# A Hymba encoder block on one core: part of the softmax shift moved from VectorE to accumulating DMAs, and loads moved from the GpSimd queue to the sync queue

## The chip, the cores and the metric

The kernel runs on one core of a Trainium2 chip. The metric is device time in microseconds (us) from launch to end; the median over runs counts. The span of a profiled execution is a little shorter than its time, since it runs from the first instruction to the last.

## The reference

One encoder layer over 2048 tokens and 16 meta tokens, all in float32, width 1024:

```python
h = concat([meta, x])                                   # 2064 x 1024
proj = rms_norm(h, g_mix) @ w_in                        # q (4 heads), k, v (2 heads of 128), u (512)
attn = softmax(rope(norm(q)) @ rope(norm(k)).T / sqrt(128)) @ v     # 2 query heads share a K/V head
four = real(fft2(u)) per 128-wide group, @ w_fourier
h = h + concat([rms_norm(attn), rms_norm(four)]) @ w_out
h = h + square(relu(rms_norm(h) @ w_up)) @ w_down       # 1024 -> 4096 -> 1024
out = rms_norm(h, g_final)[16:]
```

## The kernel before, in words

The work comes in stages: norm and input projections (until about 310 us of the profile), Fourier transform, output projection of the Fourier half (`out_f`), output projection of the attention half (`out_a`), and the MLP in two passes over 1024 tokens each (from about 1020 us), with seven products in place of eight blocks (forms "1" to "7", in `ORDER = "1265734"`). Most products are three float32r matmuls of high and low parts (`mm3`, lines 80 to 82).

Attention runs beside Fourier, `out_f` and `out_a`. It has 16 units: a unit is 256 query positions of two query heads that share one K/V head, so 512 columns. Its 2048 keys are 16 tiles of 128, held transposed (keys in the partitions): eight pairs, each one tile `S` of 128x1024, and a short tile for the meta tokens. For a unit:

- `scores`: three matmuls per key tile into a PSUM bank (two banks, tag "S"), a ScalarE copy into the half of `S` (L780), and once per pair a running maximum on VectorE (`M`, L783 and L786).
- `stats`: the maximum over keys by transposes (`pm_m`, `pd_m`), copied by ScalarE to `mb` (128x512, the same row in all partitions, L811).
- `softmax`: per pair a subtraction of `mb` on VectorE (L840), the exponential on ScalarE (L841), an addition into `acc` on VectorE (L845, L847) and four matmul passes with V into `o` (L849).
- `finish`: sums over keys, reciprocal, scaling, and a store to DRAM (`o_d`).

The scores of the next unit are computed while the softmax of the present one goes on. There are 11 buffers of `S`, eight of which one unit fills.

A scheduler of the framework sets the order on each engine's queue from the program's order and its own estimates; every queue then runs strictly in order. Five queues matter: PE (TensorE), DVE (VectorE), ACT (ScalarE), POOL (GpSimd: small tensor operations, and DMAs that it issues) and SP (sync: DMAs alone). Before, q, K (`kt`), V (`vn`, `vm`) of the units are loaded from DRAM by DMAs on POOL, since their tiles have another type (float32r) than the DRAM tensors. POOL also computes the reciprocal roots (`rs_f`, `rs_m`, `ers`) by which `out_f`, `out_a` and the final norm scale.

Between the two MLP passes, the second pass's seven operand forms of 2 MB each (`bf_tile`, from `f_d`) are loaded: six on SP, form 7 on POOL. Form 7's tile shares its memory (tag "e0") with rows of the first pass that are still being normed and stored at that time (`ers`, L1452; stores L1462 on POOL).

Of the kernel before, what the change touches and what calls it, by code (L numbers as in the profile page):

```python
# [13 lines left out]
AF = mybir.ActivationFunctionType  # L14
ALU = mybir.AluOpType
# [4 lines left out]
P = 128  # L20
# [11 lines left out]
NT = SEQ // P  # L32
# [3 lines left out]
MR = 96  # L36
# [13 lines left out]
P_BUFS = 5  # L50
S_BUFS = 11
A_BUFS = 5
ORDER = "1265734"
ISQ = 1.0 / math.sqrt(HD)


def f32v(ap):
    return ap.bitcast(F32)
# [26 lines left out]
def ins_of(x):  # L85
    return getattr(x, "ins", x)


def bc(ap, shape):
    return ap.broadcast_to(shape)  # L90
# [45 lines left out]
def encoder_block(ctx: ExitStack, tc: tile.TileContext, x, meta, w_in, w_f,  # L136
                  w_out, w_up, w_down, g_fin, g_cols, g_rows, c_id, c_rope, c_dft, c_even, c_odd, c_rem, out):
    nc = tc.nc
# [56 lines left out]
    q_d = [dram.tile([P, 2, NQ, 256], F32, name=f"q_d{b}") for b in range(8)]  # L195
    k_d = dram.tile([P, NKV, 2, SEQ + MR], F32, name="k_d")
    v_n = dram.tile([P, NKV, NT, P], F32, name="v_n")
    v_m = dram.tile([MR, NKV, P], F32, name="v_m")
    h_d = [dram.tile([P, D], F32, name=f"h_d{t}") for t in range(NT)]
    m_d = [dram.tile([P, KT, 512], F32, name=f"m_d{b}") for b in range(4)]  # L200
    f_d = {n: dram.tile([P, 2, 4, 512], F32, name=f"f_d{n}") for n in ORDER}

# [491 lines left out]
    def misc(name, shape=(P, 512)):  # L694
        return app.tile(list(shape), F32, name=name, tag="misc")


    KC = 4 * P
    KCP = 640

    def load_k(u, g, c):
        n = KC + (MR if c == 3 else 0)
        kt = ap.tile([P, 2, KCP if c == 3 else KC], R32, name=f"kt_{u}_{c}", tag=f"KT{c // 3}", bufs=1 if c == 3 else 3)
        nc.gpsimd.dma_start(kt[:, :, :n], k_d[:, g, :, c * KC:c * KC + n])
        return kt

    def load_v(u, g, c):
        if c == 4:
            vt = ap.tile([P, P], R32, name=f"vm_{u}", tag="VM", bufs=1)
            nc.gpsimd.dma_start(vt[:MR], v_m[:, g])  # L710
        else:
            vt = ap.tile([P, 4, P], F32, name=f"vn_{u}_{c}", tag="VT", bufs=4)
            nc.gpsimd.dma_start(vt, v_n[:, g, 4 * c:4 * c + 4])
        return vt

    o_d = [dram.tile([P, 2, NQ, 512], F32, name=f"o_d{b}") for b in range(4)]
# [12 lines left out]
    def attention():  # L729
# [5 lines left out]
        def load_q(u):  # L735
            b, g = units[u]
            q = ap.tile([P, 2, 2, 256], R32, name=f"q_{u}", tag="q", bufs=2)
            nc.gpsimd.dma_start(q, q_d[b][:, :, 2 * g:2 * g + 2])
            return q.rearrange("p l h n -> p l (h n)")

        def start(u, q=None):
            q = load_q(u) if q is None else q
            state[u] = dict(q=(q[:, 0], q[:, 1]), S=[], k=KV["k", u])
# [3 lines left out]
        def loads(kind, u, c):  # L747

            if u and units[u][1] == units[u - 1][1]:
                KV[kind, u] = KV[kind, u - 1]  # L750
            else:
                KV.setdefault((kind, u), []).append((load_v if kind == "v" else load_k)(u, units[u][1], c))
# [37 lines left out]
        def over_keys(x, name, op):  # L790

            ps = misc("pm_" + name, (P, 4, P))
            for a in range(4):
                nc.tensor.transpose(ps[:, a], x[:, a * P:(a + 1) * P], ident)
            r = ap2.tile([P, 4], F32, name="mx_" + name, tag="mx", bufs=2)
            nc.vector.tensor_reduce(r, ps, axis=AX.X, op=op)
            return r

        def rows_to_cols(vec, name):

            ps = misc("pd_" + name, (P, 4, P))
            for a in range(4):
                nc.tensor.transpose(ps[:, a], bc(vec[:, a:a + 1], [P, P]), ident)
            return ps.rearrange("p a e -> p (a e)")

        def stats(u):
            s = state[u]
            r = over_keys(s["M"], f"m{u}", ALU.max)
            yield
            mb = s["mb"] = ap2.tile([P, 512], F32, name=f"mb_{u}", tag="mb", bufs=2)  # L810
            nc.scalar.copy(mb, rows_to_cols(r, f"m{u}"))  # L811

        def softmax(u, i):

            s = state[u]
            nm = f"{u}_{i}"
            vt = KV["v", u]
            if i == NT:
                S = s["S"][-1][:MR]
                nc.vector.tensor_tensor(S, S, s["mb"][:MR], op=ALU.subtract)  # L820
                nc.scalar.activation(S, S, AF.Exp, scale=ISQ)
                hi = ap2.tile([P, 512], R32, name="ph_" + nm, tag="ph", bufs=1)
                acc = s["acc"]
                nc.scalar.copy(hi[:MR], S)
                nc.vector.tensor_tensor(hi[32:64], S[32:64], f32v(hi[32:64]), op=ALU.subtract)
                sm = s["sum"] = ap2.tile([P, 512], F32, name=f"sum_{u}", tag="pl", bufs=1)
                nc.vector.tensor_tensor(sm, acc[:, 0], acc[:, 1], op=ALU.add)
                nc.vector.tensor_tensor(sm[:META], sm[:META], S[:META], op=ALU.add)
                nc.tensor.matmul(s["O"], vt[4][:MR], hi[:MR], start=False, stop=True)
                return  # L830
            j = i // 2
            S = s["S"][j]
            if i == 0:
                s["acc"] = ap2.tile([P, 2, 512], F32, name=f"acc_{u}", tag="acc", bufs=1)
                s["O"] = app.tile([P, 512], F32, name=f"o_{u}", tag="O")
            acc = s["acc"]
            p = S
            if i % 2 == 0:
                mb = s["mb"].rearrange("p (o n) -> p o n", o=1).broadcast_to([P, 2, 512])
                nc.vector.tensor_tensor(S, S, mb, op=ALU.subtract)  # L840
                nc.scalar.activation(p, S, AF.Exp, scale=ISQ)  # L841
                return
            v = vt[j // 2]
            if j == 1:
                nc.vector.tensor_tensor(acc, s["S"][0], p, op=ALU.add)  # L845
            elif j > 0:
                nc.vector.tensor_tensor(acc, acc, p, op=ALU.add)  # L847
            for e in range(2):
                nc.tensor.matmul(s["O"], v[:, 2 * j % 4 + e], p[:, e], start=i + e == 1, stop=False)  # L849

        def finish(u):
# [25 lines left out]
            else:  # L877
                for h in range(2):
                    nc.vector.tensor_tensor(sqs[b], sqs[b], O[:, h * 256:(h + 1) * 256], op=ALU.add)

        q0 = load_q(0)
        for c in range(4):
            loads("k", 0, c)
# [7 lines left out]
        def more(upto):  # L891
            while ahead[0] < min(upto, total):
                w, i = divmod(ahead[0], K)
                if i == K // 2 and w < len(units) - 1:
                    start(w + 1)
                scores(w, i)
                loads_next("k", w, i)
                ahead[0] += 1
                if i == NT:
                    later.append(stats(w))  # L900
# [6 lines left out]
        for n in range(total):  # L907
            u, i = divmod(n, K)
            for g in list(later):
                if next(g, "end") == "end":  # L910
                    later.remove(g)
            softmax(u, i)
            loads_next("v", u, i)
            if i == NT:
                later.append(finish(u))
                next(later[-1])
            more(n + 1 + K + LEADT)
            yield
# [102 lines left out]
    def a_tile(name, dt=F32):  # L1021
        return mp.tile([P, 512], dt, name=name, tag="a", bufs=A_BUFS)

# [126 lines left out]
    BT = {}  # L1150

    def bf_tile(pool, name, **kw):
        t = BT[name] = pool.tile([P, 2, 4, 512], R32, name="bf" + name, **kw)
        BF[name] = [[t[:, e, k] for k in range(4)] for e in range(2)]
# [51 lines left out]
    def up_pass(p, sp, pc, UW, ready, first, hs, beside):  # L1206
# [8 lines left out]
        for g in range(8):  # L1215
            X, Y, p1, u2, p5, C = ({} for _ in range(6))

            def keep(name, q, t):
                nc.sync.dma_start(s_d[g // 2][:, ORDER.index(name), 2 * (g % 2) + q], t)

            for name in ORDER:
                hi, lo = ready.pop(0)
# [81 lines left out]
    def down_pass(p, sp, FIRST, hs):  # L1304
# [36 lines left out]
        def down_operands():  # L1341

            for g in range(4):
                raw, S, loads = {}, {}, []

                def stationary(name):
                    S[name] = []
                    for h in range(2):
                        r = dn.tile([P, 2, 512], F32, name=f"a{name}_{p}_{g}_{h}", tag="ar", bufs=a_bufs)
                        eng = nc.sync if g else nc.gpsimd  # L1350
                        loads[:] = [ins_of(eng.dma_start(r, s_d[g][:, ORDER.index(name), 2 * h:2 * h + 2]))]
                        S[name].append(r)
# [119 lines left out]
        for g in range(4):  # L1472
            X, Y = {}, {}
            last = g == 3
            for name in ORDER:
                (a0, b0), (a1, b1) = (lambda f: ((f[0], f[1]), (f[2], f[3])))(ready.pop(0))
# [134 lines left out]
    for name in "2165347":  # L1611
        if name == "7":
            bf_tile(ey, name, tag="e0")
        else:
            bf_tile(bfb, name)
    nc.gpsimd.dma_start(f32v(BT["7"]), f_d["7"])
    behind = nc.sync.dma_start(f32v(BT["1"]), f_d["1"])
    for name in "2U6534":
        with tc.issue_after(ins_of(behind)):
            if name == "U":  # L1620
                ready.append(next(UW))
            else:
                behind = nc.sync.dma_start(f32v(BT[name]), f_d[name])
# [109 lines left out]
```

## Time and profile before

| what | value |
|---|---|
| time, median of 3 runs | 2276.55 us (2273.15 to 2279.17) |
| profiled execution: time, span | 2273.03 us, 2271.2 us |
| busy: PE, DVE, ACT, POOL | 99%, 75%, 52%, 11% of the span |
| granted TensorE clock | 0.997 |
| DMA: queue q1 (issued by SP) | 307.98 MB, 40.1% of 16 engines |
| DMA: queue q0 (issued by POOL) | 57.37 MB, 8.0% of 16 engines |

Busy times come from one profiled execution. Matmuls are pipelined and their ends are modelled, so "PE busy" also holds a little waiting. A group's row reads: line, engine, operation, output<-inputs, shapes, count, busy us, mean ns of one, and the idle time of that engine just before it with what ended it.

### The profile page before, as it was taken

The numbers are of one execution on the slowest core, as the hardware profiler recorded it, in microseconds if no ns is written. First come the engines' busy times: TensorE is split into PE (matmuls) and PEld (weight loads), VectorE is DVE, ScalarE is ACT, GpSimd is POOL, SyncE is SP. The second block draws the span as 40 slices with busy tenths as digits, with TensorE's granted clock in tenths as the row PEclk, the third lists the DMA queues.
The fourth block names the chain that finished last, engine by engine and source line by source line (L and its number), as shares of the span: only waits on it lengthen the run. The fifth ranks groups of instructions, "written<-read, shape, count | busy, mean of one in ns | idle before, by whom it ended". The sixth has DMA issues, their size and how long they took to land.

```text
span 2271.2 us, 28115 instructions
## 1 busy us (share of the span) xinstructions
PE 2238.5 (99%) x10238; PEld 1772.9 (78%) x10238; DVE 1693.4 (75%) x2250; ACT 1178.0 (52%) x1997; POOL 245.6 (11%) x286
## 2 busy tenths in 40 slices
PE   9999999999999999999999999999989999999998
PEld 7888987766667666677888878888878888788887
DVE  6334589999999888888676769679655656696795
ACT  6443356665555566668555644334445555443343
POOL 2212120003223122010000020000100000200000
PEclk9999999999999999999999999999999999999999
DMA  6332252133343524367767575444674444864442
GB/s 204 88 107 78 76 156 81 51 94 113 102 154 117 193 87 136 126 255 241 254 223 247 210 268 194 159 129 148 234 304 166 154 152 154 307 200 158 127 138 84
DMA packets 191786, 367.40 MB, mean 162 GB/s; under 512 B 15760, under 2 KB 74768, under 8 KB 189984
## 3 DMA queue, kind: packets, MB, share of 16 engines
q1 hardware_dynamic: 170896, 307.98, 40.1%
q0 software_dynamic: 20608, 57.37, 8.0%
q8 instruction: 80, 1.31, 0.2%
q14 instruction: 58, 0.48, 0.1%
q10 hardware_dynamic: 144, 0.26, 0.0%
HBM read 236.28 MB, written 129.27 MB: 161 GB/s over the span
## 4 chain that ended last, share of the span: by engine, by line
PE 87%; DVE 6%; ACT 2%; issue 2%; POOL 1%; DMA 1%; SPq 0%; POOLq 0%; DVEq 0%; ACTq 0%
PE o L849 7%; PE ux L82 5%; PE ux L80 5%; PE ux L81 5%; PE dx L80 5%; PE dx L81 5%; PE dx L82 5%; PE uy L82 4%; PE uy L80 4%; PE uy L81 4%; PE dy L82 4%; PE dy L81 4%; PE dy L80 4%; PE s L80 2%; PE s L82 2%; PE s L81 2%
## 5 line engine op out<-in xcount | busy, mean ns | idle before, releaser
L70 ACT CAST ah<-a 128x1024 fp32r<-128x1024 f32 x108 | 112.9, 1049 | 261.3 <-PE dx L81 105.6
L849 PE MATMUL o<-S,vn 128*128 128x512 f32 x512 | 243.6, 596 | 3.7 <-ACT S L841 3.0
L80 PE MATMUL dx<-bh,ah 128*128 128x512 f32 x496 | 192.7, 388 | 1.3 <-DVE hs L1493 1.3
L780 ACT COPY S<-s 128x512 f32<-128x512 f32 x256 | 145.2, 585 | 92.4 <-PE s L82 72.8
L82 PE MATMUL dx<-bh,al 128*128 128x512 f32 x496 | 192.6, 388 | 0.0
L81 PE MATMUL dx<-bl,ah 128*128 128x512 f32 x496 | 192.5, 388 | 0.0
L80 PE MATMUL ux<-bf,wuh 128*128 128x512 f32 x448 | 175.5, 392 | 6.8 <-ACT wuh L70 6.8
L82 PE MATMUL ux<-bf,wul 128*128 128x512 f32 x448 | 175.0, 391 | 0.0
L81 PE MATMUL ux<-bf,wuh 128*128 128x512 f32 x448 | 175.0, 391 | 0.0
L840 DVE TENSOR_TENSOR S<-S,mb 128x1024 f32<-128x1024 f32 x128 | 155.4, 1229 | 11.9 <-ACT mb L811 11.8
L841 ACT ACTIVATE S<-S 128x1024 f32<-128x1024 f32 x128 | 135.1, 1063 | 43.0 <-DVE S L840 41.8
L80 PE MATMUL dy<-bh,ah 128*128 128x512 f32 (+1 forms) x388 | 151.2, 390 | 3.5 <-ACT ah L70 3.5
L82 PE MATMUL dy<-bh,al 128*128 128x512 f32 (+1 forms) x388 | 151.4, 390 | 1.6 <-DVE al L71 1.6
L71 DVE TENSOR_TENSOR al<-a,ah 128x1024 fp32r<-128x1024 f32 x108 | 131.3, 1220 | 27.1 <-ACT ah L70 26.8
L81 PE MATMUL dy<-bl,ah 128*128 128x512 f32 (+1 forms) x388 | 151.0, 389 | 0.0
L849 PEld LDWEIGHTS o<-S,vn 128*128 128x128 f32 x512 | 92.1, 189 | 74.6 <-issue 59.0
L80 PE MATMUL s<-q,kt 128*128 128x512 f32 (+1 forms) x272 | 145.2, 534 | 2.2 <-ACT S L780 1.9
L71 DVE TENSOR_TENSOR bl<-d,bh 128x1024 fp32r<-128x1024 f32 x92 | 112.1, 1219 | 20.2 <-ACT bh L70 20.1
L80 PE MATMUL uy<-bf,wuh 128*128 128x512 f32 x320 | 125.0, 391 | 0.3 <-ACT wuh L70 0.3
L82 PE MATMUL uy<-bf,wul 128*128 128x512 f32 x320 | 124.6, 390 | 0.7 <-DVE wul L71 0.7
L81 PE MATMUL uy<-bf,wuh 128*128 128x512 f32 x320 | 124.8, 390 | 0.0
L786 DVE TENSOR_TENSOR M<-M,S 128x1024 f32<-128x1024 f32 x96 | 117.6, 1225 | 9.0 <-ACT S L780 7.9
(324 smaller groups left out, 5658.1 us busy)
## 6 DMA issues: line engine op xcount, KB each, us to landing
a<-s_d SPq DMA_DIRECT2D x84, 512.0 KB, 3.7
R<-in_w_up_dram SPq DMA_DIRECT2D x32, 1024.0 KB, 5.4
s_d<-s SPq DMA_DIRECT2D x128, 256.0 KB, 2.1
s_d<-c SPq DMA_DIRECT2D x96, 256.0 KB, 2.7
d<-in_w_down_dram SPq DMA_DIRECT2D x48, 512.0 KB, 5.0
f_d<-lf SPq DMA_DIRECT2D x56, 256.0 KB, 2.8
a<-s_d POOLq DMA_DIRECT2D x24, 512.0 KB, 5.6
bf<-f_d SPq DMA_DIRECT2D x6, 2048.0 KB, 13.6
```

What stands on the lines that cost most here:

```text
L70: self.high = nc.scalar.copy(hi, src)
L71: self.low = nc.vector.tensor_tensor(lo, src, f32v(hi), op=ALU.subtract)
L80: nc.tensor.matmul(out, a[0], b[0], start=first, stop=False, skip_group_check=chain)
L81: nc.tensor.matmul(out, a[0], b[1], start=False, stop=False, skip_group_check=chain)
L82: nc.tensor.matmul(out, a[1], b[0], start=False, stop=last, skip_group_check=chain)
L780: nc.scalar.copy(S[:, i % 2], ps)
L786: nc.vector.tensor_tensor(M, M, S, op=ALU.max)
L840: nc.vector.tensor_tensor(S, S, mb, op=ALU.subtract)
L841: nc.scalar.activation(p, S, AF.Exp, scale=ISQ)
L849: nc.tensor.matmul(s["O"], v[:, 2 * j % 4 + e], p[:, e], start=i + e == 1, stop=False)
```

## The change

The copy of the maxima stores them negated. Behind it, POOL issues five DMAs per unit; each adds `mb`, read twice over by a broadcast, to one pair of score tiles in place (pairs 3 to 7 of the eight, `FAR = 3`). VectorE adds the negated maxima to pairs 0 to 2 and the meta tile as before. The loads of q, K, V and of form 7 move to SP; form 7 now stands between forms 5 and 3.

```diff
+FAR = 3
     def load_k(u, g, c):
-        nc.gpsimd.dma_start(kt[:, :, :n], k_d[:, g, :, c * KC:c * KC + n])
+        nc.sync.dma_start(f32v(kt[:, :, :n]), k_d[:, g, :, c * KC:c * KC + n])
     def load_v(u, g, c):
-            nc.gpsimd.dma_start(vt[:MR], v_m[:, g])
+            nc.sync.dma_start(f32v(vt[:MR]), v_m[:, g])
-            nc.gpsimd.dma_start(vt, v_n[:, g, 4 * c:4 * c + 4])
+            nc.sync.dma_start(vt, v_n[:, g, 4 * c:4 * c + 4])
         def load_q(u):
-            nc.gpsimd.dma_start(q, q_d[b][:, :, 2 * g:2 * g + 2])
+            nc.sync.dma_start(f32v(q), q_d[b][:, :, 2 * g:2 * g + 2])
         def stats(u):
-            nc.scalar.copy(mb, rows_to_cols(r, f"m{u}"))
+            nc.scalar.activation(mb, rows_to_cols(r, f"m{u}"), AF.Copy, scale=-1.0)
+            for S in s["S"][FAR:NT // 2]:
+                nc.gpsimd.dma_start(S, bc(mb.rearrange("p (o n) -> p o n", o=1), [P, 2, 512]), accum_op=ALU.add)
         def softmax(u, i):
-                nc.vector.tensor_tensor(S, S, s["mb"][:MR], op=ALU.subtract)
+                nc.vector.tensor_tensor(S, S, s["mb"][:MR], op=ALU.add)
             if i % 2 == 0:
-                mb = s["mb"].rearrange("p (o n) -> p o n", o=1).broadcast_to([P, 2, 512])
-                nc.vector.tensor_tensor(S, S, mb, op=ALU.subtract)
+                if j < FAR:
+                    mb = bc(s["mb"].rearrange("p (o n) -> p o n", o=1), [P, 2, 512])
+                    nc.vector.tensor_tensor(S, S, mb, op=ALU.add)
                 nc.scalar.activation(p, S, AF.Exp, scale=ISQ)
...
-    nc.gpsimd.dma_start(f32v(BT["7"]), f_d["7"])
     behind = nc.sync.dma_start(f32v(BT["1"]), f_d["1"])
-    for name in "2U6534":
+    for name in "2U65734":
```

ScalarE's queue in unit 9, before. A name such as `S_9_6` is unit 9, key tile 6, so pair 3; an even key tile names its pair. The list begins with pair 1's exponential; between it and the copy of unit 9's maxima stand, in both kernels, four copies and pair 0's exponential.

```order
L841 ACTIVATE S_9_2_6248<-S_9_2_6248 128x1024
L841 ACTIVATE S_9_4_6318<-S_9_4_6318 128x1024
L70 CAST ohl_8_6649<-O_8_6589 128x512
L780 COPY S_10_4_6663<-s_10_4_6659 128x512
L780 COPY S_10_4_6663<-s_10_5_6667 128x512
L872 ACTIVATE O_8_6589<-O_8_6589 128x512
L780 COPY S_10_6_6682<-s_10_6_6678 128x512
L841 ACTIVATE S_9_6_6357<-S_9_6_6357 128x1024
L70 CAST yh_13_6747<-UA_69 128x256 x2
L841 ACTIVATE S_9_8_6378<-S_9_8_6378 128x1024
L780 COPY S_10_6_6682<-s_10_7_6708 128x512
L841 ACTIVATE S_9_10_6421<-S_9_10_6421 128x1024
```

The same place after:

```order
L845 ACTIVATE S_9_2_6253<-S_9_2_6253 128x1024
L845 ACTIVATE S_9_6_6362<-S_9_6_6362 128x1024
L845 ACTIVATE S_9_4_6323<-S_9_4_6323 128x1024
L845 ACTIVATE S_9_8_6383<-S_9_8_6383 128x1024
L71 CAST ohl_8_6654<-O_8_6594 128x512
L845 ACTIVATE S_9_10_6425<-S_9_10_6425 128x1024
L781 COPY S_10_4_6668<-s_10_4_6664 128x512
L876 ACTIVATE O_8_6594<-O_8_6594 128x512
L781 COPY S_10_4_6668<-s_10_5_6672 128x512
L845 ACTIVATE S_9_12_6465<-S_9_12_6465 128x1024
L845 ACTIVATE S_9_14_6481<-S_9_14_6481 128x1024
L781 COPY S_10_6_6687<-s_10_6_6683 128x512
```

The exponentials of pairs 3 to 7 have moved ahead: all five now stand before the copy of the next unit's key tile 6. Before, none of them did: pair 3's came just behind that copy, and the others later.

POOL's queue around unit 9's accumulations, before and then after. The other rows are `out_f`'s sums of squares (`ysq`) and reciprocal roots (`rs_f`).

```order
L704 DMA kt_10_3_6526<-k_d_110 128x2x608
L738 DMA q_11_6717<-q_d5_107 128x2x512
L192 TENSOR_TENSOR rs_f_6562<-ms_f_6560,mhalf_100 128x1
L954 TENSOR_TENSOR ysq_13_6749<-ysq_13_6749 128x256
L954 TENSOR_TENSOR ysq_13_6749<-ysq_13_6749 128x128
L713 DMA vn_10_0_6676<-v_n_111 128x512
L192 TENSOR_TENSOR rs_f_6703<-ms_f_6701,mhalf_100 128x1
```

```order
L193 TENSOR_TENSOR rs_f_6562<-ms_f_6560,mhalf_100 128x1
L958 TENSOR_TENSOR ysq_13_6753<-ysq_13_6753 128x256
L958 TENSOR_TENSOR ysq_13_6753<-ysq_13_6753 128x128
L814 DMA S_9_6_6362<-mb_9_6565 128x2x512
L814 DMA S_9_8_6383<-mb_9_6565 128x2x512
L814 DMA S_9_10_6425<-mb_9_6565 128x2x512
L814 DMA S_9_12_6465<-mb_9_6565 128x2x512
L814 DMA S_9_14_6481<-mb_9_6565 128x2x512
L193 TENSOR_TENSOR rs_f_6708<-ms_f_6706,mhalf_100 128x1
```

The loads are gone from this queue, and the five accumulations stand together, in the place of a V load, with a reciprocal root behind them.

Between the MLP passes, POOL's queue before, and SP's queue after:

```order
L1452 TENSOR_TENSOR ers_0_5_14039<-epm_0_5_11838,mhalf_100 128x1
L1616 DMA bf7_14104<-f_d7_137 128x4096
L1462 DMA out_dram<-hs0_1_11930 128x512 x2
L1452 TENSOR_TENSOR ers_0_6_14060<-epm_0_6_11839,mhalf_100 128x1
L1452 TENSOR_TENSOR ers_0_7_14081<-epm_0_7_11840,mhalf_100 128x1
```

```order
L1626 DMA bf6_14100<-f_d6_135 128x4096
L1626 DMA bf5_14101<-f_d5_136 128x4096
L1626 DMA bf7_14104<-f_d7_137 128x4096
L1626 DMA bf3_14102<-f_d3_138 128x4096
L1626 DMA bf4_14103<-f_d4_139 128x4096
```

Form 7's load has left its place ahead of the last two `ers` on POOL and stands ahead of forms 3 and 4 on SP.

## The prediction

> **What bounds the kernel now.** I read the page first, then a table of windows over the attention stage, since what the change takes away lies there.
>
> ```profile
> PE 2238.5 (99%) x10238; PEld 1772.9 (78%) x10238; DVE 1693.4 (75%) x2250; ACT 1178.0 (52%) x1997; POOL 245.6 (11%) x286
> ```
>
> TensorE is busy nearly always. The windows (length, busy us of PE, PEld, DVE, ACT, POOL with counts, clock, DMA share, GB/s) say how near a second engine comes:
>
> ```profile
> 344.00:420.00 76.00, 75.62 (x354) 53.33 (x353) 73.37 (x89) 48.79 (x77) 7.03 (x11) 1.00 0.26 71
> 420.00:480.00 60.00, 59.92 (x288) 42.60 (x287) 59.32 (x75) 38.04 (x60) 0.73 (x1) 1.00 0.15 44
> 480.00:540.00 60.00, 57.76 (x243) 37.92 (x242) 58.43 (x73) 38.87 (x66) 8.78 (x10) 1.00 0.43 129
> 540.00:600.00 60.00, 59.10 (x224) 38.84 (x223) 58.49 (x72) 34.35 (x60) 25.93 (x21) 1.00 0.35 115
> ...
> 660.00:720.00 60.00, 60.00 (x241) 42.14 (x240) 55.34 (x71) 36.30 (x61) 17.30 (x16) 1.00 0.47 149
> ...
> 960.00:1020.00 60.00, 58.91 (x267) 42.84 (x266) 50.21 (x72) 38.80 (x65) 8.87 (x7) 1.00 0.63 239
> sum 676.00, PE 668.48 PEld 461.36 DVE 619.96 ACT 416.22 POOL 126.17; mean PE 60.77 PEld 41.94 DVE 56.36 ACT 37.84 POOL 11.47
> ```
>
> DVE is at 97% to 99% between 420 and 600 us, but PE still fills 668.48 of 676 us. So freeing DVE can bring back at most 7.5 us. The waits of PE in 344 to 1020 us show how much of that DVE causes:
>
> ```profile
> PE o L849 <- ACT S L841: 3.0, 5, 1.1
> PE s L80 <- ACT S L780: 1.9, 5, 0.8
> PE pm_m L794 <- DVE M L775: 1.0, 2, 0.7
> ```
>
> The first and the third, 4.0 us, hang on DVE (an exponential waits for its subtraction); I count 4 us.
>
> A second place is the change between the MLP passes. In order: PE, ACT and POOL there, then the time to landing of form loads on SP and of the one on POOL.
>
> ```profile
> 1651.66 0.39 PE L81 MATMUL uy<-bf,wuh 128*128 128x512 f32 x1
> 1651.88 0.39 PE L82 MATMUL uy<-bf,wul 128*128 128x512 f32 x1
> 1659.06 0.79 PE L80 MATMUL ux<-bf,wuh 128*128 128x512 f32 x1 [6.79 <-ACT wuh L70]
> ...
> 1652.49 1.33 ACT L1459 ACTIVATE hs<-hs,ers 128x512 f32<-128x512 f32 x2 [9.55 <-POOL ers L1452]
> ...
> 1650.22 0.58 POOL L1616 DMA_DIRECT2D bf<-f_d  x1 [9.85 <-DMA out_dram<-hs]
> ...
> DMA to landing us min/median/max: 8.4/13.6/21.9
> ...
> DMA to landing us min/median/max: 15.9/15.9/15.9
> ```
>
> POOL stands 9.85 us before form 7's load, until stores have landed; `ers` waits behind it, ACT stands 9.55 us for `ers`, and PE 6.79 us for operands behind that on ACT.
>
> **The change, part by part.** *Removed from DVE:* five of eight subtractions per unit.
>
> ```profile
> L840 DVE TENSOR_TENSOR S<-S,mb 128x1024 f32<-128x1024 f32 x128 | 155.4, 1229 | 11.9 <-ACT mb L811 11.8
> L780 ACT COPY S<-s 128x512 f32<-128x512 f32 x238 | 135.1, 584 | 89.7 <-PE s L82 71.0 <-PE o L849 5.6 <-DVE acc L847 4.7
> L841 ACT ACTIVATE S<-S 128x1024 f32<-128x1024 f32 x128 | 135.1, 1063 | 43.0 <-DVE S L840 41.8
> L872 ACT ACTIVATE O<-O 128x512 f32<-128x512 f32 x16 | 10.0, 626 | 3.1 <-DVE ohl L71 2.3 <-DVE at L71 0.8
> L70 ACT CAST ohl<-O 128x512 fp32r<-128x512 f32 x14 | 8.7, 620 | 6.1 <-DVE O L861 6.0
> L952 ACT ACTIVATE ysq<-UA 128x256 f32<-128x256 f32 x16 | 6.1, 432 | 0.0
> L70 ACT CAST yh<-UA 128x256 fp32r<-128x256 f32 x16 | 5.9, 420 | 4.6 <-PE pof L81 4.6
> ```
>
> 16 x 5 x 1.229 = 98 us of DVE go, of which 4 us are on the path. The negated copy of `mb` and the additions in place of subtractions have the same shapes; I cost them at nothing.
>
> *Form 7's load leaves POOL:* `ers` is no longer held, so up to 6.8 us return. What is late next: SP must now wait for the same stores (until 1650 us), with form 3's and 4's loads and the stores of `c` behind it. PE, without its gap, would need form 7 some 11 us after 1652 (two forms of 24 matmuls, which start 0.22 us apart) and form 3 at 1668. Form 7, issued at 1650, lands 8.4 to 15.9 us later, at 1658.6 to 1666, and form 3 behind it. So between 0 and 6.8 us are gained; I take 4.
>
> *Loads of q, K and V from POOL to SP:* what they waited for on POOL now holds SP.
>
> ```profile
> L704 POOL DMA_DIRECT2D kt<-k_d x20 | 14.5, 727 | 96.1 <-PE s L82 85.7 <-DMA k_d<-kt 10.3
> L738 POOL DMA_DIRECT2D q<-q_d x16 | 11.9, 741 | 113.3 <-PE s L82 113.1
> L713 POOL DMA_DIRECT2D vn<-v_n x20 | 11.5, 577 | 86.5 <-PE o L849 63.3 <-PE pa L567 17.4 <-PE pof L81 5.8
> ```
>
> Behind them on SP stand `out_f`'s input loads and stores, `o_d` and later `h`. Their order on SP follows the same work on PE that the loads wait for, so I take 0. Between the ends: a V load waits 86.5/20 = 4.3 us on average, so the 16 input loads of `out_f`, if each stood that long and nothing covered it, would cost 69 us; leaving POOL free for `rs_f` cannot gain more than the 7.5 us above.
>
> *Added: 80 accumulating DMAs.* No such DMA is in this trace. POOL's issue I price as a load's, 0.73 us, 58 us in all against 41 us of loads removed; POOL is at 19% (126 of 676 us), so this is covered, unless a reciprocal root comes late behind it. What counts is when each lands, for the exponential waits for it, and behind that wait on ACT the next unit's score copies, and behind those PE.
>
> When are they wanted? From the end of `mb`'s copy ACT has, by its order after, four copies and an exponential (3.4 us), pair 1's exponential, then pair 3's at 4.5 us; with pair 2's between, pair 4's at 6.6; pair 5's at 8.3, pair 6's at 11.1, pair 7's at 12.2. Then a score copy, and PE has two score banks only. ACT also waits for PE in between. For this, unit 9 before, on ACT:
>
> ```profile
> 702.91 0.59 ACT L811 COPY mb<-pd_m 128x512 f32<-128x512 f32 x1 [1.22 <-PE pd_m L803]
> ...
> 705.05 1.08 ACT L841 ACTIVATE S<-S 128x1024 f32<-128x1024 f32 x1
> ...
> 706.48 2.25 ACT L841 ACTIVATE S<-S 128x1024 f32<-128x1024 f32 x2
> ...
> 715.59 1.06 ACT L841 ACTIVATE S<-S 128x1024 f32<-128x1024 f32 x1 [0.62 <-DVE S L840]
> ...
> 727.54 2.20 ACT L841 ACTIVATE S<-S 128x1024 f32<-128x1024 f32 x2
> ```
>
> Before, the last exponential began at 728.6, 25.1 us after the copy of `mb` ended at 703.5; its place in the queue, counted in the same way (twelve copies, seven exponentials, six smaller operations: 7.0 + 7.4 + 3.0), is 17.4 us. So waits stretch the queue by 25.1/17.4 = 1.44, and pair 7 after is wanted between 12.2 and 1.44 x 12.2 = 17.6 us.
>
> When do they land? Here are POOL's queue on the page (packets, MB, share of 16 engines) and the landing of the q loads, 512 KB each as an accumulation writes:
>
> ```profile
> q0 software_dynamic: 20608, 57.37, 8.0%
> ...
> DMA to landing us min/median/max: 4.3/4.8/8.7
> ```
>
> 57.37 MB in 8.0% of 2271.2 us are 0.316 MB per us: 1.66 us for 512 KB, so 4.8 - 1.66 = 3.1 us lie around the transfer. The low end of the price is this plain rate: five in a row land at 4.8, 6.4, 8.1, 9.8 and 11.4 us after `mb`, each within 0.3 us of the earliest it is wanted. For the high end, an accumulation reads two operands (`mb` and `S`) where a load reads one: twice the time, 3.3 us, if reading sets the pace. Then they land at 6.4, 9.7, 13.0, 16.3 and 19.6 us, the last 2.0 to 7.4 us late. I take the doubled rate, because nothing in the rows lets an engine read two streams in the time of one, and 4 us per unit, a little under the middle, because an ACT that is late waits less for PE. The stall passes to PE whole: it is at 99%, so the time cannot be made up later in the unit. 16 x 4 = 64 us.
>
> The Trainium skill, "Collectives: The Full Stack", section "The bandwidth ceiling: the fold count and why AG ≠ RS ≠ AR", says that an add inside the DMA engines costs no cycles of its own but two source reads on one ring, and gives 62.28 against 32.35 GB/s for a copy and a reduction. No run here shows it yet. By its ratio of 1.93 an accumulation would take an estimated 3.2 us and the sum would be some 8 us lower than mine (five transfers, 16 units, 0.1 us each); by a plain copy's rate it would be that of the first rival.
>
> *Sum.* 2273.03 - 4 (DVE's waits) - 4 (form 7) + 64 = 2329 us for an execution like the profiled one. The median before is 3.5 us above that execution, so about 2332 us.
>
> **The rivals.** *Landing in time (faster).* The accumulations run at the plain rate and only the gains are left. For it: the DMA engines are used to 15% to 47% through most of the stage, and `o` for pair 7 comes late in a unit. Against it: the two reads. It gives 2276.55 - 8 = 2268.5 us, and at most 2276.55 - 7.5 - 6.8 = 2262. It decides for faster if one accumulation takes less than about 1.85 us: at 1.9 us the fifth lands at 12.6, 0.4 us late, and 16 x 0.4 = 6 of the 8 us are gone.
>
> *Nothing gained or lost.* The fifth is late by about half a us per unit: 16 x 0.5 = 8 us give the gains back, 2276 us. PE at 668.48 of 676 us speaks for it, since there is so little to win.
>
> *Far too late.* Other transfers hold 26% to 63% of the DMA engines in these windows. If the accumulations have only the rest, say 62%, one takes 3.3/0.62 = 5.3 us, the fifth lands at 29.6 us, 12 us past even the latest that it is wanted: 16 x 12 = 192 us, about 2460 us. Against it: the first units run at a DMA share of 0.15 to 0.26.
>
> *SP becomes the wait.* A K or V load that waits for PE holds `out_f`'s input behind it: 4.3 us on average and at most 69 us in all, as above, 2276.55 - 8 + 69 = 2338. It would look like the forecast in time, but PE would wait for `xo` and not for `S`. I give it little, since these loads wait for PE's own progress.
>
> **How the numbers follow.** Late by a few us (forecast, 2300 to 2390 us): 0.40. Far too late (over 2390 us): 0.14. SP's wait: 0.04. Nothing gained or lost: 0.13. In time: 0.29. A difference of 0.3%, 6.8 us, is about what a measurement of this kernel can tell from none; slower by more than that has 0.40 + 0.14 + 0.04 = 0.58, the same 0.13, faster 0.29. The range reaches from 2262 us, the most that the gains can give, to 2430 us, where the accumulations are 10 us late in each unit; about 2 in 10 are left outside, nearly all above. The likeliest case alone has 2300 to 2390 us.
>
> **What would show it.** The first and the last of the 16 copies of the maxima before:
>
> ```profile
> 344.86 0.59 ACT L811 COPY mb<-pd_m 128x512 f32<-128x512 f32 x1 [0.39 <-PE pd_m L803]
> ...
> 957.39 0.59 ACT L811 COPY mb<-pd_m 128x512 f32<-128x512 f32 x1 [1.43 <-PE pd_m L803]
> ```
>
> Right: on the page after, L845 (the exponential) on ACT has idle time before it ended by DMA S<-mb, some 4 us in each of 16 units; the period from one copy of `mb` to the next, (957.39 - 344.86)/15 = 41 us before, is 45 us; accumulations issued together land over 3 us apart; PE's waits for ACT in the stage rise from 5 to some 60 us, and DVE's share there falls from 92% to near 70%. For form 7: no 9.85 us stand on POOL, and PE's gap at the first form 6 of the second pass is below 3 us. Wrong: accumulations land 1.7 us apart, and the exponentials do not wait for them; or the score copies between the exponentials hold ACT so long that each has landed; or PE waits for `xo`, `kt` or a reciprocal root in place of `S`.

## The result, and the profile after

The changed kernel takes 2373.18 us (median of 4 runs, 2370.24 to 2375.02) against 2275.16 us before (median of 4 runs, one more than above, 2273.15 to 2279.17): the ratio is 1.0426 with a 95% interval of 1.0412 to 1.0439, 98 us slower. The profiled execution spans 2368.5 us.

Its page, engines and POOL's DMA queue (packets, MB, share of 16 engines):

```profile
PE 2268.4 (96%) x10238; PEld 1791.5 (76%) x10238; DVE 1611.4 (68%) x2170; ACT 1179.6 (50%) x1997; POOL 270.1 (11%) x304
...
q0 software_dynamic: 30272, 72.36, 14.0%
```

DVE's busy time fell by 82 us (the 80 subtractions gone took 98.8 us by their own records, but neighbouring records on DVE overlap), and PE went from 99% to 96% busy. PE's busy time grew by 30 us as well, with the same 10238 matmuls. To find the place, take the stretch from the first copy of `mb` to the last, 15 units, before (columns: length; busy us of PE, PEld, DVE, ACT, POOL with counts; granted clock; DMA share; GB/s):

```profile
345.00:958.00 613.00, 606.57 (x2510) 416.00 (x2509) 567.64 (x700) 376.09 (x624) 117.31 (x109) 1.00 0.36 115
```

and after:

```profile
348.00:1056.00 708.00, 633.18 (x2515) 432.10 (x2513) 490.78 (x626) 376.16 (x624) 145.97 (x135) 0.95 0.62 155
```

The stretch is 95.0 us longer, which is nearly the whole loss. It has two parts. PE's idle time rose from 613.00 - 606.57 = 6.4 to 708.00 - 633.18 = 74.8 us, 68.4 us more. And PE was busy 26.6 us longer with nearly the same matmuls (2515 and 2510), at a granted clock of 0.95 in place of 1.00. The waits name the idle time; after, PE in that stretch:

```profile
PE s L81 <- ACT S L781: 57.9, 18, 9.4
PE o L853 <- ACT S L845: 13.1, 6, 4.4
```

and, from the page, what ACT's exponential was waiting for:

```profile
L845 ACT ACTIVATE S<-S 128x1024 f32<-128x1024 f32 x128 | 133.8, 1062 | 110.6 <-DMA S<-mb 103.3
```

PE waits for a free score bank, the bank waits for ACT's copy, and that copy is queued on ACT behind an exponential that waits for an accumulation. Unit 9 after shows the chain, ACT first:

```profile
761.73 0.60 ACT L812 ACTIVATE mb<-pd_m 128x512 f32<-128x512 f32 x1 [1.17 <-PE pd_m L804]
...
769.07 2.01 ACT L845 ACTIVATE S<-S 128x1024 f32<-128x1024 f32 x2 [2.69 <-DMA S<-mb]
771.63 1.06 ACT L845 ACTIVATE S<-S 128x1024 f32<-128x1024 f32 x1 [0.55 <-DMA S<-mb]
772.59 0.60 ACT L71 CAST ohl<-O 128x512 fp32r<-128x512 f32 x1
774.52 1.06 ACT L845 ACTIVATE S<-S 128x1024 f32<-128x1024 f32 x1 [1.33 <-DMA S<-mb]
775.49 0.57 ACT L781 COPY S<-s 128x512 f32<-128x512 f32 x1
...
780.56 1.06 ACT L845 ACTIVATE S<-S 128x1024 f32<-128x1024 f32 x1 [2.41 <-DMA S<-mb]
```

Four of the five accumulations find ACT already waiting. The copy at 775.49 is what PE was standing for. PE at that moment, in the same unit:

```profile
776.11 0.50 PE L81 MATMUL s<-q,kt 128*128 128x512 f32 x1 [3.65 <-ACT S L781]
776.44 0.57 PE L82 MATMUL s<-q,kt 128*128 128x512 f32 x1
776.81 0.63 PE L83 MATMUL s<-q,kt 128*128 128x512 f32 x1
777.24 0.63 PE L81 MATMUL pof<-wfh,yh 128*128 128x512 f32 x1
777.67 0.63 PE L82 MATMUL pof<-wfl,yh 128*128 128x512 f32 x1
...
780.09 0.39 PE L82 MATMUL pof<-wfl,yh 128*128 128x512 f32 x1
780.32 0.39 PE L83 MATMUL pof<-wfh,yl 128*128 128x512 f32 x1
```

Here is the second part: after the 3.65 us pause the matmuls start 0.43 us apart until 779.8, and 0.23 us apart from 780.1 on. The granted clock (the column behind the counts) says the same of these two stretches:

```profile
776.50:779.90 3.40, 3.40 (x10) 2.63 (x9) 3.23 (x4) 1.62 (x3) 0.00 (x0) 0.50 1.08 218
780.00:783.40 3.40, 3.40 (x15) 2.34 (x14) 2.43 (x5) 2.84 (x6) 0.56 (x1) 1.00 0.54 170
```

By the trace's clock records the clock is 0.50 in twelve pieces of the long stretch, 68.3 us together, and in none of it before. Each of PE's eleven pauses of 3.06 us or more has such a piece at its end or just behind it; the twelfth stands behind a pause of 1.97 us. PE is busy 52.4 us inside the pieces; half of that, 26.2 us, is time that matmuls at the full clock would not have taken, close to the 26.6 us.

On POOL, the five accumulations of that unit, and the distance from issue to landing over all 80:

```profile
762.74 3.71 POOL L814 DMA_DIRECT2D S<-mb  x3 [0.59 <-ACT mb L812]
769.30 1.20 POOL L814 DMA_DIRECT2D S<-mb  x1 [2.85 <-issue]
771.86 1.20 POOL L814 DMA_DIRECT2D S<-mb  x1 [1.35 <-issue]
...
DMA to landing us min/median/max: 5.2/9.1/15.5
```

Three go out at once, the fourth 2.9 us behind the third, when the first has landed. From the end of `mb`'s copy the five land at 5.7, 9.0, 12.1, 15.7 and 18.9 us (medians over the 16 units, worked out from each landing in the trace). Form 7, last, at PE's first form 6 of the second MLP pass (6.79 us of waiting before):

```profile
1753.69 0.80 PE L81 MATMUL ux<-bf,wuh 128*128 128x512 f32 x1 [3.11 <-ACT wuh L71]
```

### The profile page after: what moved, and what is told of

Its sections match the earlier page's. It is cut to its first block, busy times and chain, and to the rows that moved or that the text cites. A ratio compares the mean times of both kernels' runs of the same rounds, so it can differ in the third digit from the quotient of the medians.

```text
span 2368.5 us, 28176 instructions
## 1 busy us (share of the span) xinstructions
PE 2268.4 (96%) x10238; PEld 1791.5 (76%) x10238; DVE 1611.4 (68%) x2170; ACT 1179.6 (50%) x1997; POOL 270.1 (11%) x304
## 4 chain that ended last, share of the span: by engine, by line
PE 64%; DMA 6%; DVE 3%; issue 3%; ACT 2%; POOL 0%; SPq 0%; POOLq 0%; ACTq 0%; DVEq 0%
DMA S<-mb 5%; PE dx L83 5%; PE dx L82 5%; PE dx L81 5%; PE ux L83 5%; PE ux L81 4%; PE ux L82 4%; PE o L853 4%; PE dy L83 4%; PE dy L81 4%; PE dy L82 4%; PE uy L83 3%; PE uy L81 3%; PE uy L82 3%; PE s L81 1%
## 5 line engine op out<-in xcount | busy, mean ns | idle before, releaser
L853 PE MATMUL o<-S,vn 128*128 128x512 f32 x512 | 250.3, 610 | 14.1 <-ACT S L845 14.0
L81 PE MATMUL s<-q,kt 128*128 128x512 f32 (+1 forms) x272 | 153.0, 562 | 61.6 <-ACT S L781 57.9
L845 ACT ACTIVATE S<-S 128x1024 f32<-128x1024 f32 x128 | 133.8, 1062 | 110.6 <-DMA S<-mb 103.3
L81 PEld LDWEIGHTS s<-q,kt 128*128 128x128 f32 (+1 forms) x272 | 52.5, 193 | 106.3 <-ACT S L781 75.7
L814 POOL DMA_DIRECT2D S<-mb x80 | 98.1, 1509 | 303.4 <-ACT mb L812 195.7
L81 PE MATMUL uy<-bf,wuh 128*128 128x512 f32 x320 | 125.0, 391 | 0.3 <-ACT wuh L71 0.3
L72 DVE TENSOR_TENSOR bl<-d,bh 128x1024 fp32r<-128x1024 f32 x92 | 112.1, 1220 | 19.2 <-ACT bh L71 18.9
## 6 DMA issues: line engine op xcount, KB each, us to landing
bf<-f_d SPq DMA_DIRECT2D x7, 2048.0 KB, 12.5
```

What stands on the lines that cost most here:

```text
L72: self.low = nc.vector.tensor_tensor(lo, src, f32v(hi), op=ALU.subtract)
L81: nc.tensor.matmul(out, a[0], b[0], start=first, stop=False, skip_group_check=chain)
L814: nc.gpsimd.dma_start(S, bc(mb.rearrange("p (o n) -> p o n", o=1), [P, 2, 512]), accum_op=ALU.add)
```

## The experiments

My theory: each accumulation reads twice what a copy reads, so five of them land some 3 us apart, behind the places that the schedule gave their exponentials on ACT; the moves to the sync queue cost nothing. The rivals: the loads on SP, the accumulations' traffic on the DMA engines, POOL's descriptor ring, or the new order on ACT by itself. Ratios are against the kernel before, on the same chip.

### Which part of the change costs the time

All additions on DVE, everything else as changed:

```diff
-FAR = 3
+FAR = 8
```

> The changed kernel with FAR = 8: no accumulation, all eight additions of a unit on DVE; the loads of q, K, V and form 7 stay on SP and the negated copy stays. Theory (the accumulations land too late, the loads' move is free): about 2269 to 2276 us, some 3 us under before from form 7, no wait of L845 on ACT for DMA, period of the mb copies back at 41 us. Rival (the loads on SP, or the traffic they bring on SP's queue, hold the attention): 2330 to 2370 us, with PE or ACT waiting for kt, vn or xo. An even split would be near 2325.

Measured: 2272.83 us, ratio 0.9990 (0.9981 to 0.9999), and 40.6 us from one copy of `mb` to the next. And form 7's move alone, on the kernel before:

```diff
-    nc.gpsimd.dma_start(f32v(BT["7"]), f_d["7"])
-    for name in "2U6534":
+    for name in "2U65734":
```

> The kernel before with form 7's load moved from POOL to SP, between forms 5 and 3, and nothing else. Theory: PE's gap at the first form 6 of the second pass goes from 6.8 to about 3.1 us and a gap of about 1 us comes at form 7: 2272 to 2274 us against 2275, a gain of 2.5 to 3.5 us, 0.1%. Rival (SP's stores and form 3 come late behind it): no gain or up to 5 us lost.

Measured: 2271.98 us, ratio 0.9987 (0.9978 to 0.9995), 1 to 5 us gained, the lowest median of these runs. PE's two gaps stand where they were expected:

```profile
1656.61 0.80 PE L80 MATMUL ux<-bf,wuh 128*128 128x512 f32 x1 [3.11 <-ACT wuh L70]
1689.07 0.50 PE L82 MATMUL ux<-bf,wul 128*128 128x512 f32 x1 [0.69 <-DVE wul L71]
```

The two runs differ by 0.9 us, less than either interval is wide: the moves of q, K and V cost nothing in sum that can be measured. The accumulations cost all of it, 2373.2 - 2272.8 = 100 us.

### What makes an accumulation slow

Plain copies in their place, with the same program on every engine:

```diff
-  nc.gpsimd.dma_start(S, bc(mb..., [P, 2, 512]), accum_op=ALU.add)
+  nc.gpsimd.dma_start(S, bc(mb..., [P, 2, 512]))
```

> The changed kernel with its 80 accumulating DMAs turned into plain copies of the same shape and place (S is overwritten by mb, so the softmax is left out of what is computed; the program on every engine is instruction for instruction the same). Theory (two reads per accumulation set the pace): packets of 2048 bytes at about 98 ns in place of 184, copies about 1.7 us apart while several are in flight, the fifth at about 11 to 12 us after mb in place of 18.9, and the time 2268 to 2290 us. Rival (ACT's new order alone, or any 512 KB transfer inside SBUF in this place, costs the time): packets still near 184 ns or the period still 47 us, and 2350 to 2373 us.

Measured: 2278.84 us, ratio 1.0018 (1.0008 to 1.0028), the fifth copy landing at 10.4 us (median). ACT hardly waits for them:

```profile
ACT S L845 <- DMA S<-mb: 14.1, 9, 4.2
```

The order on ACT is the changed kernel's, so that order and the copies' traffic together cost 6 us (over the run with all additions on DVE), not 100. The first 20 us of unit 9 after, as the DMA engines saw it (busy tenths in 40 slices, then the queues):

```profile
DMA  0019379999999999999999999999999999999993
...
q0 software_dynamic: 1360, 2.62, 74.4%
q1 hardware_dynamic: 835, 1.31, 23.6%
```

and the first 12 us of the same unit with plain copies, which took POOL's queue just as many bytes:

```profile
q0 software_dynamic: 720, 2.62, 58.1%
q1 hardware_dynamic: 501, 0.87, 29.1%
```

So five accumulations hold the 16 engines for 0.744 x 19.7 = 14.7 us, 2.9 us each, and five copies for 0.581 x 11.7 = 6.8 us, 1.4 us each. With the additions 33 of the 40 slices, 16 us, are at 9 tenths or more. The same bytes cost 2.15 times as much with the addition. That the second read is what doubles the price is my reading; no run here separates it from the rest of what the addition does. The Trainium skill, "Collectives: The Full Stack", section "The bandwidth ceiling: the fold count and why AG ≠ RS ≠ AR", has two source reads for an add and a ratio of 1.93, measured there on collectives between cores; the trace agrees in kind, and the ratio here is a little higher.

The packets' sizes differed, though, which I had not expected: 2048 bytes with the addition (184 ns, median) and 4096 without (173 ns). To tell size from addition, each copy was cut in two:

```diff
-  nc.gpsimd.dma_start(S, bc(mb..., [P, 2, 512]), accum_op=ALU.add)
+  for e in range(2):
+      nc.gpsimd.dma_start(S[:, e], mb)
```

> The run with plain copies in place of accumulations, but each as two copies of 256 KB, so that the packets are 2048 bytes as those of the accumulations were (again S is overwritten, so the softmax is left out of what is computed). Theory (an accumulation costs a second read): a 2048-byte packet takes about 90 to 100 ns against 184 with the addition, the last copy of a unit lands by 12 to 13 us after mb, and the time is 2272 to 2290 us. Rival (the small packets cost it, not the addition): about 184 ns a packet, the last copy near 18 us, 2340 us or more.

Measured: 2278.44 us, ratio 1.0014 (1.0004 to 1.0023), the last copy landing at 11.3 us (median). But the packets came as 4096 bytes again (10240 of them, 172 ns), so this run did not test what it was made for. What speaks against the size is the kernel before: its 2048-byte packets on the same queue, loads from DRAM without an addition, took 99 ns (median). They come from DRAM and not from SBUF, so this speaks against the size without settling it.

POOL's ring, which held three accumulations, was the next suspect:

```diff
-dynamic_dma_scratch_size=2048
+dynamic_dma_scratch_size=4096
```

> The changed kernel with twice the memory for POOL's DMA descriptors (4096 for 2048), every engine's program the same. In the changed kernel POOL begins the fourth accumulation of a unit some 6 us after mb, when the first has landed, and the fifth near 9 us. Theory (the rate of the transfers, about 3 us each, sets the landings): all five are issued by 7 us, the fifth lands at 17 to 18 us in place of 18.9, and the time is 2350 to 2373 us. Rival (the wait for room in POOL's ring makes them late): the fifth lands by 14 us and the time falls below 2330 us.

Measured: 2375.51 us, ratio 1.0434 (1.0417 to 1.0450). All five now go out together; on POOL, and the distance to landing:

```profile
481.35 6.17 POOL L814 DMA_DIRECT2D S<-mb  x5 [40.72 <-ACT mb L812]
...
DMA to landing us min/median/max: 5.4/10.9/19.5
```

The fourth and fifth, issued 3.4 and 6.0 us earlier, land no sooner: the five come at 5.9, 9.0, 12.5, 15.7 and 19.0 us after `mb`. I had expected the last at 17 to 18, so even that was too much: the wait on POOL cost nothing, the transfers are the limit.

### Whether the exponentials stood too early

Two accumulations only:

```diff
-FAR = 3
+FAR = 6
```

> The changed kernel with FAR = 6: accumulations for pairs 6 and 7 alone, POOL's ring never full. The schedule again gives the exponentials of these pairs early places on ACT: pair 6's is third, about 3.7 us after mb, pair 7's follows at about 9 us. Theory (each exponential is put ahead of its landing): pair 6 lands at 5.7 and is 2.0 us late, pair 7 lands at 8.5 and is in time; 16 x 2.0 = 32 us less what PE does not need, 2285 to 2305 us. Rival (the late ones are only the fourth and fifth in the ring): 2270 to 2276 us, as with none.

Measured: 2304.27 us, ratio 1.0126 (1.0112 to 1.0139), at the upper end of what the theory gave. The ring never fills here, and yet ACT waits:

```profile
ACT S L845 <- DMA S<-mb: 42.9, 18, 7.0
```

Pair 7, which I had expected in time, accounts for ten of these eighteen waits (by the landings in the trace). The schedule puts whatever is accumulated forward: pair 6's exponential stands third on ACT, ahead of pair 2's. Then the reverse, all five accumulations, with the exponentials where before had them:

```diff
+LATE = {3: 3, 4: 8, 5: 8, 6: 8, 7: 11}   # pair: score copy of the next unit
-            nc.scalar.copy(S[:, i % 2], ps)
+            s.setdefault('cp', {})[i] = ins_of(nc.scalar.copy(S[:, i % 2], ps))
...
+                with tc.issue_after(w["cp"][LATE[j]]) if w and j in LATE else nullcontext():
+                    nc.scalar.activation(p, S, AF.Exp, scale=ISQ)
```

> The changed kernel with all its accumulations, but the exponentials of pairs 3 to 7 placed on ACT where before had them (behind the copies 3, 8, 8, 8 and 11 of the next unit's score tiles). Theory (the accumulations are only late for the early places that the schedule gave the exponentials): before reached pair 4 at 12.1 us and pair 7 at 25.1 us after mb, the accumulations land at 8.5 and 18.9 us, so the stall goes: 2265 to 2280 us, L845's idle time for DMA under 15 us in all (from 103). Rival (the traffic of 80 accumulations slows everything, or POOL's queue does): 2340 us or more, whatever the order; halfway, if pair 5 to 6 at 12 to 15 us stay late behind pair 4, 2290 to 2320.

Measured: 2292.95 us, ratio 1.0075 (1.0061 to 1.0089): 80 of the 100 us come back with the same 80 accumulations. That misses my range of 2265 to 2280 and lies at the low end of the halfway case, and ACT's idle time for accumulations is 27.8 us where I had put it under 15:

```profile
ACT S L848 <- DMA S<-mb: 27.8, 12, 7.5
```

Four of these twelve waits stand in the last unit, which has no next one to place the exponentials by; the other eight stand at the first accumulation to land, pair 3's, and not at pairs 5 and 6 as the halfway case had it. Two runs tell this from a price of the traffic. With pair 3 back on DVE (`FAR = 4`, the same places for pairs 4 to 7):

> FAR = 4 and the exponentials of pairs 4 to 7 placed on ACT where before had them (behind the copies 8, 8, 8 and 11 of the next unit's score tiles); pair 3 is subtracted on DVE again. In the run with five late ones the rest of ACT's waits for accumulations stood almost all at pair 3, which lands at 5.7 us or later. Theory: no wait of L845's exponentials for DMA over 5 us in all but in the last unit, which has no next one, and 2268 to 2276 us. Rival (what was left, 18 us, is the traffic of the accumulations): a fifth less than it, 2286 to 2290 us.

Measured: 2275.41 us, ratio 0.9999 (0.9990 to 1.0008). No exponential waits for an accumulation but in the last unit. ACT's wait for late weights (`wfr`, of the output projection) and the wait of PE behind it:

```profile
ACT wfh L75 <- DMA wfr<-in_w_out_dram: 7.1, 2, 6.5
...
516.16 0.79 PE L82 MATMUL s<-q,kt 128*128 128x512 f32 x1 [5.37 <-ACT S L782]
```

With pair 3 kept, but its exponential moved back further (`LATE = {3: 6, 4: 8, 5: 8, 6: 9, 7: 11}`):

> All five accumulations, with the exponentials of pairs 3 to 7 placed behind the copies 6, 8, 8, 9 and 11 of the next unit's score tiles, so that pair 3's, too, comes long after its landing. Theory (place alone): 2268 to 2277 us. Rival (the accumulations' traffic costs some 18 us wherever the exponentials stand): 2288 to 2295 us.

Measured: 2287.32 us, ratio 1.0057 (1.0044 to 1.0069). Here my theory failed: outside the first and the last unit ACT waits 1.2 us for accumulations, and 12 us are still lost against before, close to what the rival gave. ACT's waits for DMA in this run, PE's longest wait, and the time to landing of the weights `wfr`:

```profile
ACT S L848 <- DMA S<-mb: 11.8, 8, 1.9
...
ACT wfh L75 <- DMA wfr<-in_w_out_dram: 9.6, 2, 5.8
...
524.08 0.79 PE L82 MATMUL s<-q,kt 128*128 128x512 f32 x1 [8.21 <-ACT S L782]
...
DMA to landing us min/median/max: 2.5/5.6/12.3
```

In unit 4 the weights `wfr`, loaded on SP, come late: they land up to 12.3 us after their issue, at most 4.2 us with all additions on DVE. ACT, in order, stands 9.6 us for them, and PE 8.2 us behind ACT. With all additions on DVE ACT waited 0.7 us for these weights in all, before 1.6. That wait of PE is 8.2 of the 14.5 us by which this run lies over the one with all additions on DVE; another 2.3 us of PE's waiting stand in the first unit, and the rest is not traced to a cause. So the loss needs both the slow accumulations and the early places: over the run with all additions on DVE, copies in the early places cost 6 us, all five accumulations in late places 14 to 20. Early places on ACT were the larger part of the 100 us. That crowded DMA engines are a second, smaller part is read from these traces (the run with four accumulations has 7.1 us of it on `wfh`); no run takes the crowding away alone.

## Why the prediction was right, and where it was off

It said slower by a stall behind late accumulations, 2332 us; measured 2373. The mechanism was right, and the loss of 98 us was forecast at 55. The term that was too small is the lateness per unit, 4 us where ACT stood 6.5. Its steps in turn:

- *DVE's relief, 4 us:* not seen. With four accumulations and no waits for them the time is that of before, 2275.4 us, form 7's gain included. If the 4 us were there, PE's wait of 5.4 us for late weights in that run took them.
- *Form 7, 4 us:* alone it gave 2.8 us (1 to 5). The 9.85 us on POOL are gone; PE's gap went to 3.11 us where I had it below 3. In the changed kernel the part behind the attention has the old length all the same, so there the gain does not show.
- *Loads on SP, nothing:* right in sum, 0.9 us between the two runs. PE does wait 3.0 us for one K load as attention begins (3.5 us in the changed kernel), which it did not before; with all additions on DVE the stretch behind it is 3.6 us shorter. The rival that SP becomes the wait is out.
- *POOL's issue at 0.73 us:* mis-sized. An accumulation takes 1.22 us and the ring holds three, but the doubled ring showed that none of this costs time.
- *The accumulation at 3.3 us for 512 KB:* 2.9 us measured. The landings forecast at 6.4, 9.7, 13.0, 16.3 and 19.6 us came at 5.7, 9.0, 12.1, 15.7 and 18.9. The low end, 1.66 us, was a copy's price (1.4 us here); with it the rival "landing in time" would have had its landings, and the run with copies had 2278.8 us.
- *Late by 4 us per unit:* the mechanism was right, the size too small. ACT's idle time for accumulations was to be some 4 us in each unit and came to 103.3/16 = 6.5. Between 2.0 and 7.4 us I took a little under the middle, with the reason that a late ACT waits less for PE. That reason failed: ACT's idle time in the stretch that these DMAs did not end, 237 us before, was still 234 after. The fifth landed 18.9 - 12.2 = 6.7 us behind the place that ACT's own work gives it, so the place without stretching fits what was measured. With 6.5 in place of 4 the sum would have been 2332 + 40 = 2372 us.
- *"The stall passes to PE whole":* in sum, yes: the period of `mb` grew by 6.3 us, nearly ACT's 6.5. But on PE only 68.4/15 = 4.6 us of that are idle time. The other 26.6/15 = 1.8 us are matmuls at half the clock behind the pauses, a thing that the prediction does not have. That its 4 us lie so near PE's 4.6 us of idle time is luck: it had put all of the loss there. (4.6 + 1.8) x 16 = 102 us are what the accumulations cost.

The slow matmuls could be read in the trace before, in rows just behind one that I quoted, the gap at 1659 us:

```profile
1661.34 0.63 PE L81 MATMUL ux<-bf,wuh 128*128 128x512 f32 x1
1661.77 0.63 PE L82 MATMUL ux<-bf,wul 128*128 128x512 f32 x1
...
1664.05 0.39 PE L80 MATMUL ux<-bf,wuh 128*128 128x512 f32 x1
1664.29 0.39 PE L81 MATMUL ux<-bf,wuh 128*128 128x512 f32 x1
```

There, too, matmuls stood 0.43 us apart behind the gap, and 0.23 us apart from 1663.4 us on. The Trainium skill, "TensorE: Matmul & The Clock Gate", section "What's actually happening", says that an idle window of about 3.4 us halves TensorE's clock, and that about 3.4 us of sustained work restore it. The trace agrees (0.43 against 0.23 us, for some 3.7 us after 776.4), and here pauses from 3.06 us on were enough. No run here took the slow clock away by itself: that PE spent 26.6 us more under it is measured, that the kernel would be as much faster without it is not.

Of what would show it, the period of `mb` came out at 47.1 us (45 forecast), DVE's share in the stretch at 490.78/708 = 69% (near 70%), PE's waits for ACT at 71 us (some 60). "Far too late" did not come: the median of the fifth landing is 18.9 us. But its reason, other transfers in the way, holds in single units: in unit 11, where SP's queue took 93% of the engines for 5.7 us behind `mb`, the five landed at 11.3 to 23.0 us.

## What to carry to other kernels

Taking work off an engine that was not the bound bought nothing here, and what replaces it must arrive before the in-order engine that consumes it gets there: compare each landing with the consumer's place in its queue, and look whether the schedule has moved the consumer forward. An addition inside a DMA cost about twice a copy of the same bytes, and while several ran, other loads came late too. When a stall reaches TensorE, do not look for all of it in idle time: here 26.6 us of slow matmuls came with 68.4 us of idle time.

## What the runs showed of the hardware

- An accumulating DMA from SBUF to SBUF moves in 2048-byte packets of 184 ns; a plain one of the same shape in 4096-byte packets of 173 ns.
- POOL takes 1.22 us to issue an accumulation, 0.72 us for the copy of the same shape; 2048 bytes of descriptor memory hold three accumulations or all five copies.
- More accumulations in flight do not land sooner: 18.9 us after `mb` for the fifth with three in flight, 19.0 with five.
- Each of PE's eleven pauses of 3.06 to 9.39 us in the attention stage came with a granted clock of 0.50 for 3.4 to 10.2 us at its end or just behind it, with matmuls 0.43 us apart in place of 0.23.
